# Seven block products in place of eight in the up-projections of a feed-forward layer

## The chip, the cores and the metric

The program runs on one core of a Trainium2 chip. Five engines work beside each other, each through its own queue in a fixed order: TensorE (PE in the profile, with PEld for the loads of its stationary operands), VectorE (DVE), ScalarE (ACT), GpSimd (POOL) and SyncE (SP), which here only issues DMAs. The metric is the device time of one execution in microseconds (us): the median of several runs.

## The reference

One inference step of an encoder trunk with two layers, over 640 tokens: 512 frames of a new stream, and 16 frames each of 8 running streams. The width is 1024. The first layer mixes by chunked spatial gating beside a gated convolution, the second by attention with forget gates. Each layer then has a feed-forward part, and that is what the change is about. All in float32:

```python
def _conv_ffn(x, prev, w_up, conv_w, w_down):       # x is normed; w_up (1024, 5632), w_down (2816, 1024)
    z, st = _causal_dwconv(x @ w_up, conv_w, prev)   # width 3, along time; prev: the streams' last two rows
    gate, up = jnp.split(z, 2, axis=-1)
    return (jax.nn.silu(gate) * up) @ w_down, st
...
    hp = _rmsnorm(xp, norm_ffn[layer])
    yp, st_p = _conv_ffn(hp, zero_f, w_up[layer], conv_ffn[layer], w_down[layer])
    xp = xp + yp
```

The same is done for the running streams, with their states. The last rows of `x @ w_up` are outputs too, as the new state.

## The kernel before

**Layout.** Activations are kept with features on the 128 partitions and tokens along the free axis: `x` is 8 chunks of 128x640. Weights are the stationary operand of TensorE, tokens move. A product of a float32 weight and a float32 activation is made of three float32r products: each operand is split into a high part (a cast) and a low part (what the cast left out), and high x high, high x low and low x high are accumulated in PSUM. A matmul has 320 tokens, half of them all, and the two halves lie on the two sides of a PSUM bank border. So one output block of 128 features costs 8 chunks x 3 x 2 = 48 matmuls.

**Weights.** `weights()` (L83 to L90) loads 128x1024 float32 (512 KB) by a DMA that SP issues into `raw` (L87), casts the high part `whi` on ACT (L88) and subtracts the low part `wlo` on DVE (L89). Each of the three has a ring of three buffers.

**The norm.** The operands `hh` and `hl` of the up-projection are x times the norm's gain g only. The root `rb`, a number for each token, is multiplied in when a product leaves PSUM.

**The feed-forward layer.** `ffn()` walks over 22 units. Unit j (`up(j)`) is output block j of the gate and block 22+j of the up half: 96 matmuls (L109). Then, for each of the two blocks, `pad_evac` takes the block from PSUM times `rb` into a padded buffer `zp` (DVE L190, L191; POOL L183 puts the old state in), `new_state` copies the last two columns of each stream (POOL L202), and `conv` makes three taps (ACT L196, DVE L198 twice). The gate goes through silu (ACT L355); the product (DVE L358, L359) is split again (ACT L97, DVE L98) and becomes an operand of the down-projection.

The down-projection is done in parts, since its contraction runs over all units: `PARTS` lists units 0 to 5, 6 to 11, 12 to 16 and 17 to 21. After each part (and the first unit of the next) `project` runs through the eight output blocks, with 6 matmuls for each unit of the part, and adds each block to x (DVE L209). The block that ends the program is halved by tokens (`last_block`, L327).

**PSUM.** The pool `pm` has three tiles of two banks, tag `mm`; two more banks are the pool behind `aux()`.

**What sets the order.** A scheduler walks through the program as written, with a model of durations, and writes a fixed order for each engine's queue. On the chip each queue runs in that order; semaphores make it wait for the others. An instruction that waits holds back everything behind it in its own queue.

Of the kernel before, what the change touches and what calls it, by code (L numbers as in the profile page):

```python
# [8 lines left out]
F32 = mybir.dt.float32  # L9
# [34 lines left out]
# columns of the constants of the attention  # L44
# [4 lines left out]
NS = 256 + 16      # keys of a stream  # L49


class Core:
    def __init__(self, ctx, tc, io):
# [5 lines left out]
        self.wp = pool(ctx, "wts", bufs=3)  # L59
        self.hp = pool(ctx, "hp", bufs=8)  # L60
        # 4 norms x 8 chunks
# [8 lines left out]
        self.n = 0  # L70

# [4 lines left out]
    # ---- weights: float32 from DRAM, split exactly into two float32r parts  # L76
    def weights(self, src, cols=1024, pieces=1, between=None):
        nc = self.nc
        raw = self.wp.tile([P, 1024], F32, tag="raw", name=self.nm("raw"))
# [12 lines left out]
    def split(self, pool, tags, src):  # L92
        """float32 [128, 640] -> (hi, lo) float32r tiles"""
        nc = self.nc
        hi = pool.tile([P, T], F32R, tag=tags[0], name=self.nm("sh"))
        lo = pool.tile([P, T], F32R, tag=tags[1], name=self.nm("sl"))
        nc.scalar.copy(out=hi, in_=src)  # L97
        nc.vector.tensor_tensor(out=lo, in0=src, in1=hi.bitcast(F32), op=ALU.subtract)  # L98
        return hi, lo

    # ---- products, weights stationary, tokens moving
# [10 lines left out]
    def psum(self):  # L112
        return self.pm.tile([P, 1024], F32, tag="mm", name=self.nm("mm"))
# [11 lines left out]
    # ---- RMS norm: operands scaled by g now, by the root later  # L125
# [28 lines left out]
    def stats(self, acc, pool, aux):  # L154
        """1/rms for each token, as columns [128, 5]"""
# [8 lines left out]
    def spread(self, rt, pool, aux):  # L164
        """columns [128, 5] -> the same along the free axis of every partition"""
# [727 lines left out]
```

## Time and profile before

| | |
|---|---|
| median of 3 runs | 1534.07 us (1534.03 to 1534.29) |
| the profiled execution's span, first to last instruction | 1531.9 us |
| granted TensorE clock in it, mean | 1.000 |
| first mixer | to about 200 us |
| feed-forward of layer 0 | about 227 to 680 us |
| attention | about 680 to 1076 us |
| feed-forward of layer 1 | about 1076 to 1532 us |

The profile is of one execution, 2.2 us shorter by its span than the median. Its page gives the busy time of each engine, the chain of work that ended last and the groups of instructions by line. A view of waits lists what an engine waited for; a view by stretches gives busy times within a stretch; a timeline lists single instructions with start and length. In the names of instructions stands output <- inputs, then partitions x elements.

### The profile page before, as it was taken

The numbers are of one execution on the slowest core, as the hardware profiler recorded it, in microseconds if no ns is written. First come the engines' busy times: TensorE is split into PE (matmuls) and PEld (weight loads), VectorE is DVE, ScalarE is ACT, GpSimd is POOL, SyncE is SP. The second block draws the span as 40 slices with busy tenths as digits, with TensorE's granted clock in tenths as the row PEclk, the third lists the DMA queues.
The fourth block names the chain that finished last, engine by engine and source line by source line (L and its number), as shares of the span: only waits on it lengthen the run. The fifth ranks groups of instructions, "written<-read, shape, count | busy, mean of one in ns | idle before, by whom it ended". The sixth has DMA issues, their size and how long they took to land.

```text
span 1531.9 us, 26648 instructions
## 1 busy us (share of the span) xinstructions
PE 1517.8 (99%) x11008; PEld 1473.5 (96%) x11008; DVE 899.1 (59%) x1541; ACT 559.4 (37%) x918; POOL 237.4 (15%) x281
## 2 busy tenths in 40 slices
PE   8999999999999999999999999999999999999999
PEld 6999999999999999999989888888999999999998
DVE  6545437644653655675676766768765466365463
ACT  5422334322322322345545454535432233133231
POOL 5000122201210201143111111003221021021010
PEclk9999999999999999999999999999999999999999
DMA  6222212222223222243544343523222222321313
GB/s 226 77 82 73 77 56 85 68 81 85 62 64 95 64 66 93 62 156 103 180 128 136 122 123 104 183 60 107 83 60 76 87 67 57 98 73 53 107 47 106
DMA packets 52296, 142.90 MB, mean 93 GB/s; under 512 B 6656, under 2 KB 13744, under 8 KB 52048
## 3 DMA queue, kind: packets, MB, share of 16 engines
q1 hardware_dynamic: 45424, 133.79, 28.6%
q10 hardware_dynamic: 6752, 7.41, 1.4%
q8 instruction: 87, 1.43, 0.4%
q14 instruction: 33, 0.27, 0.1%
HBM read 125.41 MB, written 11.54 MB: 89 GB/s over the span
## 4 chain that ended last, share of the span: by engine, by line
PE 96%; DVE 2%; issue 1%; ACT 1%; DMA 0%; POOL 0%; SPq 0%; DVEq 0%; ACTq 0%
PE mm L109 71%; PE pj L507 10%; PE pv L583 3%; PE po L109 2%; PE pt L576 1%; PE mm L239 1%; PE pt L662 1%; PE sc L569 1%; DVE hl L132 1%; PE sc L570 1%; DVE wlo L89 1%; PE scs L641 1%; PE pt L537 1%; PE pt L655 0%; PE scs L634 0%
## 5 line engine op out<-in xcount | busy, mean ns | idle before, releaser
L88 ACT CAST whi<-raw 128x1024 fp32r<-128x1024 f32 (+4 forms) x222 | 207.6, 937 | 494.6 <-PE mm L109 426.1
L109 PE MATMUL mm<-hl,whi 128*128 128x320 f32 x1664 | 379.4, 309 | 0.5 <-DVE hl L132 0.5
L109 PE MATMUL mm<-hh,whi 128*128 128x320 f32 x1664 | 379.8, 309 | 0.0
L109 PE MATMUL mm<-hh,wlo 128*128 128x320 f32 x1664 | 379.2, 309 | 0.0
L109 PEld LDWEIGHTS mm<-hl,whi 128*128 128x128 f32 x1664 | 278.2, 188 | 0.7 <-DVE hl L132 0.7
L109 PEld LDWEIGHTS mm<-hh,whi 128*128 128x128 f32 x1664 | 278.2, 188 | 0.1
L109 PEld LDWEIGHTS mm<-hh,wlo 128*128 128x128 f32 x1664 | 278.0, 188 | 0.0
L89 DVE TENSOR_TENSOR wlo<-raw,whi 128x1024 fp32r<-128x1024 f32 (+4 forms) x222 | 245.5, 1107 | 33.3 <-ACT whi L88 33.0
L109 PE MATMUL mm<-sh,wlo 128*128 128x320 f32 x866 | 197.2, 309 | 1.3 <-DVE wlo L89 1.3
L109 PE MATMUL mm<-sl,whi 128*128 128x320 f32 x866 | 197.2, 309 | 0.0
L109 PE MATMUL mm<-sh,whi 128*128 128x320 f32 x866 | 196.2, 309 | 0.0
L202 POOL COPY so<-zp 128x18 f32<-128x18 f32 x88 | 89.4, 1016 | 570.4 <-DVE zp L191 570.4
L190 DVE TENSOR_TENSOR zp<-mm,rb 128x512 f32<-128x512 f32 x88 | 60.9, 692 | 195.8 <-PE mm L109 195.8
L209 DVE TENSOR_TENSOR x<-mm,x 128x640 f32<-128x640 f32 x79 | 65.0, 823 | 185.6 <-PE mm L109 185.6
L198 DVE SCALAR_TENSOR_TENSOR t<-zp,cst,t 128x656 f32<-128x656 f32 x184 | 165.1, 900 | 10.3 <-ACT t L196 5.6
L109 PEld LDWEIGHTS mm<-sh,wlo 128*128 128x128 f32 x866 | 144.6, 188 | 1.6 <-DVE wlo L89 1.6
L109 PEld LDWEIGHTS mm<-sl,whi 128*128 128x128 f32 x866 | 144.8, 188 | 0.0
L109 PEld LDWEIGHTS mm<-sh,whi 128*128 128x128 f32 x866 | 144.4, 188 | 0.2 <-issue 0.2
L507 PE MATMUL pj<-wlo,hh 128*128 128x256 f32 x480 | 137.7, 287 | 0.7 <-DVE wlo L89 0.7
L507 PE MATMUL pj<-whi,hh 128*128 128x256 f32 x480 | 137.7, 287 | 0.0
L507 PE MATMUL pj<-whi,hl 128*128 128x256 f32 x480 | 137.5, 287 | 0.0
L507 PEld LDWEIGHTS pj<-wlo,hh 128*128 128x128 f32 x480 | 91.6, 191 | 2.8 <-issue 1.6
(188 smaller groups left out, 1691.3 us busy)
## 6 DMA issues: line engine op xcount, KB each, us to landing
raw<-w_up SPq DMA_DIRECT2D x88, 512.0 KB
raw<-w_dn SPq DMA_DIRECT2D x32, 384.0 KB
raw<-w_c SPq DMA_DIRECT2D x24, 512.0 KB
raw<-w_dn SPq DMA_DIRECT2D x32, 320.0 KB
raw<-w_ab SPq DMA_DIRECT2D x16, 512.0 KB
ck<-c_k SPq DMA_DIRECT2D x16, 512.0 KB
cv<-c_v SPq DMA_DIRECT2D x16, 512.0 KB
o_kv<-z ACTq DMA_DIRECT2D x8, 640.0 KB
```

Source lines behind the costliest of these rows:

```text
L88: nc.scalar.copy(out=hi[:, c], in_=raw[:, c])
L89: nc.vector.tensor_tensor(out=lo[:, c], in0=raw[:, c], in1=hi[:, c].bitcast(F32), op=ALU.subtract)
L109: nc.tensor.matmul(outs[h], lhsT=l, rhs=r[:, h * HT:(h + 1) * HT], start=start and k == 0, stop=stop and k == 2)
L132: nc.vector.scalar_tensor_tensor(out=lo, in0=x, scalar=gs, in1=hi.bitcast(F32), op0=ALU.mult, op1=ALU.subtract)
L190: nc.vector.tensor_tensor(out=op, in0=a[:, 0:TP], in1=b[:, 0:TP], op=ALU.mult)
L198: nc.vector.scalar_tensor_tensor(out=cv[:, 0:CW], in0=zp[:, i:i + CW], scalar=w[:, i:i + 1], in1=cv[:, 0:CW], op0=ALU.mult, op1=ALU.add)
L202: self.nc.gpsimd.tensor_copy(out=out.rearrange("p (s c) -> p s c", c=2), in_=zp[:, 496:ZW].rearrange("p (s c) -> p s c", c=18)[:, :, 16:18])
L209: self.nc.vector.tensor_tensor(out=x, in0=ps[:, C0:C0 + T], in1=x, op=ALU.add)
L239: nc.tensor.matmul(pvs[tb], lhsT=l[:, tb * P:(tb + 1) * P], rhs=r[:, (kc % 2) * 512:(kc % 2 + 1) * 512], start=kc == 0 and k == 0, stop=kc ...
L507: nc.tensor.matmul(out[tb], lhsT=l[:, tb * P:(tb + 1) * P], rhs=r[:, c:c + 256], start=kc == 0 and i == 0, stop=kc == 7 and i == 2)
L537: nc.tensor.transpose(t[:, tb * P:(tb + 1) * P], z[i][:, tb, pair * P:(pair + 1) * P], k.ident)
L583: nc.tensor.matmul(ov[64 * hh:64 * hh + 64, i * P:n], lhsT=z[2][:, j, (2 * pair + hh) * 64:(2 * pair + hh) * 64 + 64], rhs=u[:, j * P:(j + ...
```

## The change

The four quarters of a pair of output blocks are computed with seven products in place of eight (a form of Winograd's variant of Strassen's scheme). A unit is the matrix [gate block, up block] over K = 1024, and the moving matrix has two halves of tokens. K is cut in two by chunks: `KORD` puts the even chunks into the first half and the odd ones into the second, and `_layout` orders the rows of `w_up` so. Each product is over 4 chunks, one 320-token operand and one set of weights: 4 x 3 = 12 matmuls, 84 for the unit in place of 96.

- **Operands.** The scheme needs sums and differences of the two token halves, so the operands must be fully normed (x times g times `rb`). Units 0 to 3 (`NSTD`) stay standard, on the old operands, while `forms(j)`, written after each unit, makes two normed chunks (DVE L144) and four combinations of 320 tokens for them (DVE L148 to L151); three combinations are split into `fbh` and `fbl`. At unit 4 `settle` overwrites the old operands with the splits of the normed chunks.
- **Weights.** `pair_weights` loads the gate block (`g`) and the up block with its two halves of K swapped (`u`), splits D from the first half of `u`, then adds two more blocks from DRAM into `u` by an accumulating DMA that POOL issues (L172; the copies `w_x` are new inputs, made beside the others by reordering alone), and makes two sums on DVE (L175, L176). A, B and C are splits of 1024 columns.
- **Low parts by DMA.** `added` (L101 to L105) makes a low part as minus the high part on ACT (L103), to which a POOL-issued accumulating DMA adds the unsplit value (L104). It serves the weights of units 1 to 3 (`weights_added`), the down blocks (`weights_down`) and `fbl`. Unit 0 still uses `weights()`.
- **PSUM.** Banks X, Z and Y of a unit; ACT copies values out in between (`snap`, L204), and DVE combines them into the padded buffers (L211, L219, L220, L222). The pool `pm` becomes `pz` (two tiles) and `pd` (one); `psum()` takes turns among the three.
- **Order.** Six parts (0-3, 4-7, 8-11, 12-15, 16-18, 19-21). From unit 4 the down blocks of the previous part are written between the products of the units (`downs.pop`); the last part keeps `project`.
- **The rest.** `new_state` moves from POOL to ACT (L340). There are three `zp` instead of four, 4 `tmp`, four buffers of `whi` and `wlo`; `rb` shares a buffer with `acc`. The scratch space of GpSimd's DMAs is set to 1024.

The core of the diff:

```diff
-PARTS = ((0, 6), (6, 12), (12, 17), (17, 22))
+PARTS = ((0, 4), (4, 8), (8, 12), (12, 16), (16, 19), (19, 22))
+NSTD = 4
+KORD = (0, 2, 4, 6, 1, 3, 5, 7)
...
+    def added(self, pool, tags, raw, src, n, cols):
+        nc = self.nc
+        hi, lo = (pool.tile([P, n], F32R, tag=t, name=self.nm(t)) for t in tags)
+        nc.scalar.copy(out=hi[:, 0:cols], in_=raw)
+        nc.scalar.mul(out=lo[:, 0:cols], in_=hi[:, 0:cols].bitcast(F32), mul=-1.0)
+        nc.gpsimd.dma_start(out=lo[:, 0:cols], in_=src, accum_op=ALU.add)
+        return hi, lo
+    def weights_added(self, src):
+        raw = self.raw()
+        self.nc.sync.dma_start(out=raw, in_=src)
+        return self.added(self.wp, ("whi", "wlo"), raw, src, 1024, 1024)
+    def weights_down(self, src, cols):
+        raw = self.fx.tile([P, 512], F32, tag="dr", name=self.nm("dr"))[:, 0:cols]
+        self.nc.sync.dma_start(out=raw, in_=src)
+        return self.added(self.fd, ("dh", "dl"), raw, src, 512, cols)
...
+    def forms(self, p, x, g, rb, ring, fb):
+        ys = [pool.tile([P, T], F32, tag=t, name=self.nm("y")) for t in tags]
+        for c, y in zip((2 * p, 2 * p + 1), ys):
+            stt(out=y, in0=x[c], scalar=self.gv[:, 8 * g + c:8 * g + c + 1], in1=rb, op0=ALU.mult, op1=ALU.mult)
+        (a1, b1), (a2, b2) = ((y[:, 0:HT], y[:, HT:T]) for y in ys)
+        t = self.raw()[:, 0:3 * HT]
+        t2, t3, t4 = (t[:, i * HT:(i + 1) * HT] for i in range(3))
+        tt(out=t3, in0=b2, in1=b1, op=ALU.subtract)
+        tt(out=b1, in0=a1, in1=b1, op=ALU.subtract)
+        stt(out=t2, in0=b2, scalar=-1.0, in1=b1, op0=ALU.mult, op1=ALU.subtract)
+        stt(out=t4, in0=t2, scalar=-1.0, in1=a2, op0=ALU.mult, op1=ALU.subtract)
+        return ys, self.added(fb, ("fbh", "fbl"), t, t, 3 * HT, 3 * HT)
+    def settle(self, p, h, form):
+        ys, fb = form
+        for y, (hi, lo) in zip(ys, h):
+            self.part(hi, lo, y)
...
+    def pair_weights(self, gate, up, more):
+        g, u, v = self.raw(), self.raw(), self.raw()
+        nc.sync.dma_start(out=g, in_=gate)
+        nc.sync.dma_start(out=u, in_=up)
+        D = self.split(self.fd, ("dh", "dl"), u[:, 0:H], H)
+        nc.gpsimd.dma_start(out=u, in_=more, accum_op=ALU.add)
+        A = self.split(self.wp, w, g, 1024)
+        B = self.split(self.wp, w, u, 1024)
+        nc.vector.tensor_tensor(out=v[:, 0:H], in0=u[:, 0:H], in1=g[:, 0:H], op=ALU.add)
+        nc.vector.tensor_tensor(out=v[:, H:2 * H], in0=g[:, H:2 * H], in1=v[:, 0:H], op=ALU.add)
+        C = self.split(self.wp, w, v, 1024)
...
+    def pair_blocks(self, w, f, zg, zu, states, downs):
+        self.product(X, w["x11"], f, "y1a", True)
+        p1 = snap(X, 1.0)
+        self.product(Z, w["x12"], f, "y2a", True)
+        nc.vector.tensor_tensor(out=zg[:, 2:2 + HT], in0=Z, in1=p1, op=ALU.add)
+        self.product(X, w["s2"], f, "t2", False)
+        u = snap(X, -1.0)
+        self.product(Y, w["s3"], f, "t3", True)
+        p7 = snap(Y, -1.0)
+        if downs:
+            downs.pop(0)()
+        self.product(X, w["s1"], f, "t1", False)
+        nc.vector.tensor_tensor(out=zu[:, 2 + HT:514], in0=p7[:, 0:n], in1=X[:, 0:n], op=ALU.subtract)
...
+        self.product(Y, w["x22"], f, "t4", False)
+        nc.vector.tensor_tensor(out=zu[:, 2:2 + HT], in0=u, in1=Y, op=ALU.subtract)
+        if downs:
+            downs.pop(0)()
+        self.product(X, w["s4"], f, "y2b", False)
+        nc.scalar.copy(out=zg[:, 2 + HT:514], in_=X[:, 0:n])
...
+            for j in range(a, b):
...
+                if j < NSTD:
+                    blocks = (j, NJ + j)
+                    if j == 0:
+                        ps = self.blocks([self.weights(io["w_up"][l, i]) for i in blocks], hk, first)
+                    else:
+                        ps = [self.blocks([self.weights_added(io["w_up"][l, i])], hk)[0] for i in blocks]
...
+                else:
+                    if f is None:
+                        f = [self.settle(p, (h[2 * p], h[2 * p + 1]), forms[p]) for p in range(4)]
+                    w = self.pair_weights(io["w_up"][l, j], io["w_x"][l, j, 0], io["w_x"][l, j, 1])
+                    self.pair_blocks(w, f, zg, zu, sts, downs)
...
+                acts.append(act(zg, zu, j))
+                if j < NSTD:
+                    forms.append(self.forms(j, x, g, rb, ring, fb))
```

How the order moves is shown at the start of the first feed-forward layer. Before, ACT's queue around the end of unit 0 (`whi_264`, `whi_267` are the weights of unit 1, `whi_277`, `whi_280` those of unit 2; the L196 and L355 rows are unit 0's convolutions and silu):

```order
L88 CAST whi_267_2137<-raw_266_2136 128x1024
L88 CAST whi_277_2265<-raw_276_2264 128x1024
L196 ACTIVATE t_258_2110<-zp_2_88,cst_66 128x656
L196 ACTIVATE t_259_2119<-zp_4_90,cst_66 128x656
L355 ACT_TABLE_LOAD
L355 ACTIVATE t_258_2110<-t_258_2110 128x656
L88 CAST whi_280_2271<-raw_279_2270 128x1024
L97 CAST sh_261_2126<-t_260_2123 128x640
```

Here the casts of the weights of unit 1, and one of unit 2, stand ahead of the work on unit 0's products. After the change, ACT's queue from the end of unit 1 to the start of unit 2 (`zp_4` and `zp_2` hold unit 1's blocks, `whi_291` and `whi_295` are unit 2's weights):

```order
L340 COPY so_253_2004<-zp_2_88 128x18
L334 ACTIVATE t_280_2274<-zp_2_88,cst_66 128x656
L334 ACTIVATE t_281_2278<-zp_4_90,cst_66 128x656
L483 ACTIVATE t_281_2278<-t_281_2278 128x656
L127 CAST sh_283_2286<-t_282_2283 128x640
L102 CAST fbh_288_2299<-raw_287_2294 128x960
L102 CAST whi_291_2306<-raw_290_2304 128x1024
L103 ACTIVATE fbl_289_2300<-fbh_288_2299 128x960
L102 CAST whi_295_2362<-raw_294_2360 128x1024
L103 ACTIVATE wlo_292_2307<-whi_291_2306 128x1024
L103 ACTIVATE wlo_296_2363<-whi_295_2362 128x1024
```

The casts of unit 2's weights now stand behind unit 1's convolutions, silu, split and `fbh`, the cast of its combined operands. What `fbh` reads is made on DVE, in this order after the convolution of unit 1:

```order
L486 TENSOR_TENSOR t_282_2283<-t_281_2278,t_280_2274 128x512
L487 TENSOR_TENSOR t_282_2283<-t_281_2278,t_280_2274 128x128
L144 SCALAR_TENSOR_TENSOR y_285_2290<-x2_76,gv_64,rb_244_1974 128x640
L128 TENSOR_TENSOR sl_284_2287<-t_282_2283,sh_283_2286 128x640
L144 SCALAR_TENSOR_TENSOR y_286_2291<-x3_77,gv_64,rb_244_1974 128x640
L148 TENSOR_TENSOR raw_287_2294<-y_286_2291,y_285_2290 128x320
L149 TENSOR_TENSOR y_285_2290<-y_285_2290 128x320
L150 SCALAR_TENSOR_TENSOR raw_287_2294<-y_286_2291,y_285_2290 128x320
L151 SCALAR_TENSOR_TENSOR raw_287_2294<-raw_287_2294,y_286_2291 128x320
```

The two normed chunks (L144), which read only x, the gain and `rb`, stand behind the product of the unit. And PE after the change, from the last matmuls of unit 1 (`mm_279`) into unit 2 (`mm_293` and `mm_297`):

```order
L239 MATMUL mm_279_2217<-hh_239_1957,whi_277_2212 128x320 x2
L239 MATMUL mm_279_2217<-hl_240_1958,whi_277_2212 128x320 x2
L239 MATMUL mm_279_2217<-hh_239_1957,wlo_278_2213 128x320 x2
L239 MATMUL mm_293_2311<-hh_195_1573,whi_291_2306 128x320 x2
L239 MATMUL mm_293_2311<-hl_196_1574,whi_291_2306 128x320 x2
L239 MATMUL mm_297_2367<-hh_195_1573,whi_295_2362 128x320 x2
L239 MATMUL mm_297_2367<-hl_196_1574,whi_295_2362 128x320 x2
L239 MATMUL mm_293_2311<-hh_195_1573,wlo_292_2307 128x320 x2
```

Unit 2 begins with eight matmuls on the high parts of both its blocks, then needs the low part `wlo_292`. Nothing of another unit stands between. In all, PE has 10576 matmuls in place of 11008.

More of the change, by code (lines that the diff above doesn't have):

```diff
@@ L70, in __init__ @@
         self.n = 0
+        self.turn = -1
     def nm(self, s):
@@ new lines, in weights_added, with split @@
+    def weights_added(self, src):
+        raw = self.raw()
+        self.nc.sync.dma_start(out=raw, in_=src)
[4 more added lines that the diff above has]
+        return self.added(self.fd, ("dh", "dl"), raw, src, 512, cols)
+    def split(self, pool, tags, src, n=T):
+        nc = self.nc
+        hi = pool.tile([P, n], F32R, tag=tags[0], name=self.nm("sh"))
+        lo = pool.tile([P, n], F32R, tag=tags[1], name=self.nm("sl"))
+        self.part(hi, lo, src)
+        return hi, lo
@@ L201, in new_state @@
     def new_state(self, zp, out):
[L202 to L203 removed]
+        self.nc.scalar.copy(out=out.rearrange("p (s c) -> p s c", c=2),
+                            in_=zp[:, 496:ZW].rearrange("p (s c) -> p s c", c=18)[:, :, 16:18])
     def conv_compact(self, cv):
@@ new lines, in ffn, with act @@
+        two = lambda a, n: a.rearrange("p (u c) -> p u c", u=2)
+        def act(zg, zu, b):
+            cvs = []
+            for z, i in ((zu, 1), (zg, 0)):
+                o = O_CF + (l * NB + b + i * NJ) * 3
+                cv = self.conv(z, self.cst[:, o:o + 3])
+                if i == 0:
+                    nc.scalar.activation(out=cv[:, 0:CW], in_=cv[:, 0:CW], func=AF.Silu)
+                cvs.append(self.conv_compact(cv))
+            pr = self.tmp()
+            nc.vector.tensor_tensor(out=pr[:, 0:TP], in0=cvs[1][0], in1=cvs[0][0], op=ALU.mult)
+            nc.vector.tensor_tensor(out=pr[:, TP:T].rearrange("p (s c) -> p s c", c=16), in0=cvs[1][1], in1=cvs[0][1], op=ALU.mult)
+            return self.split(rpool, rtags, pr[:, :T])
@@ L375 @@
+        self.project([io["w_dn"][l, ob][:, a * P:b * P] for ob in range(8)], prev, None, x, finish, cols=(b - a) * P, out=out)
 class Attention:
@@ L810, in _layout @@
     d["w_oab"] = cols(a["w_out_ab"][0], 8)
-    d["w_up"] = np.stack([cols(a["w_up"][l], NB) for l in range(2)])
+    wu = np.stack([cols(a["w_up"][l].reshape(NC, P, -1)[list(KORD)].reshape(1024, -1), NB) for l in range(2)])
+    d["w_up"] = wu
+    up, gate = wu[:, NJ:], wu[:, :NJ]
+    d["w_x"] = con(np.stack([np.concatenate([up[..., 512:], up[..., :512]], -1),
+                             np.concatenate([up[..., :512], gate[..., :512]], -1)], 2))
     d["w_dn"] = np.stack([cols(a["w_down"][l], 8) for l in range(2)])
```

164 lines of the change are left out of this document (105 added, 59 removed).

## The prediction

> **What bounds the kernel now.** I read the busy shares first, then the chain that ended last, then what TensorE (PE) waited for, and then the feed-forward stages alone.
>
> ```profile
> span 1531.9 us, 26648 instructions
> PE 1517.8 (99%) x11008; PEld 1473.5 (96%) x11008; DVE 899.1 (59%) x1541; ACT 559.4 (37%) x918; POOL 237.4 (15%) x281
> PE 96%; DVE 2%; issue 1%; ACT 1%; DMA 0%; POOL 0%; SPq 0%; DVEq 0%; ACTq 0%
> ```
>
> PE works 99% of the span and carries 96% of the chain. The pieces of the chain and the waits of PE say how tightly:
>
> ```profile
> 125.26 7.04 PE mm L109 x48
> 227.19 452.76 PE mm L109 x3087
> 1076.18 447.33 PE mm L109 x3050
> ...
> PE mm L239 <- ACT hh L131: 5.7, 1, 5.7
> PE mm L239 <- DVE wlo L89: 1.6, 1, 1.6
> PE mm L109 <- DVE wlo L89: 1.3, 1, 1.3
> ```
>
> Both feed-forward stages (227 to 680 us and 1076 to 1523 us) are one unbroken run of matmuls of 128x320. The first is 452.76 us for 3087, or **146.67 ns a matmul**; one block of 48 alone, 7.04 us, gives the same. All waits of PE that are listed sum to about 11 us, half of it at the program's start. So a matmul taken out of these stages is worth its whole 146.67 ns, and a new wait of PE there costs its whole length. The view by stages shows how much room the other engines have in the first stage (the columns are the stretch, then busy us and count for PE, PEld, DVE, ACT, POOL, then granted clock, DMA share and GB/s):
>
> ```profile
> 227.00:680.00 453.00, 453.00 (x3091) 453.00 (x3090) 262.07 (x356) 151.59 (x181) 73.04 (x90) 1.00 0.27 81
> ```
>
> DVE is busy 58% of it, ACT 33%, POOL 16%, the DMA engines 27%.
>
> **The change part by part.** *Matmuls removed.* In 36 units (18 in each layer) 96 matmuls become 7 products of 12, so 12 fewer each: 432 x 146.67 ns = **-63.4 us**. The products stay at 128x320 and in PSUM, and the blocks of 48 above already show that pace within one block, so I price a remaining matmul as before.
>
> *Units from the fifth on.* A unit there has 84 matmuls and, with its share of the previous part's down blocks (eight over four units, so two blocks of 24 matmuls), 132: 19.4 us. DVE and ACT get more kinds of work, but these rows price it:
>
> ```profile
> L89 DVE TENSOR_TENSOR wlo<-raw,whi 128x1024 fp32r<-128x1024 f32 x140 | 173.3, 1240 | 28.6 <-ACT whi L88 28.3
> L198 DVE SCALAR_TENSOR_TENSOR t<-zp,cst,t 128x656 f32<-128x656 f32 x184 | 165.1, 900 | 10.3 <-ACT t L196 5.6
> L88 ACT CAST whi<-raw 128x1024 fp32r<-128x1024 f32 x140 | 146.7, 1049 | 325.7 <-PE mm L109 264.9 <-issue 39.6 <-PE aux L239 10.7
> L209 DVE TENSOR_TENSOR x<-mm,x 128x640 f32<-128x640 f32 x79 | 65.0, 823 | 185.6 <-PE mm L109 185.6
> L97 ACT CAST sh<-t 128x640 fp32r<-128x640 f32 x52 | 37.8, 727 | 137.6 <-DVE t L359 120.8 <-DVE t L279 9.5 <-DVE t L300 7.3
> L358 DVE TENSOR_TENSOR t<-t,t 128x512 f32<-128x512 f32 x44 | 30.5, 693 | 1.7
> L774 DVE TENSOR_TENSOR x<-po,x 128x320 f32<-128x320 f32 x16 | 7.4, 486 | 1.3 <-PE po L109 1.1
> ```
>
> DVE: three subtractions of 1024 and one of 512, two sums of 512, four evacuations of up to 320, four convolution steps, the product, one split and two additions to x: 3.7+0.7+1.4+1.7+3.6+1.0+0.8+1.6 = 14.5 us, 75% of 19.4. ACT: four casts, five copies of PSUM, two convolution starts, silu, the split and two down blocks at two casts each: about 12 us, 63%. Neither becomes the bound. Every wait that the order gives PE there has cover: the addition of `more` into `u` (L172) has 53 to 121 matmuls of earlier work between its release and its reader (mostly 71 or more, 10 us), the low parts of the down blocks 65 or more (9.5 us). The raw buffers turn over in about 12.2 us plus one accumulating transfer, against 19.4 us. I price the units at nothing, as long as such a transfer takes under 7 us; without that cover each microsecond above it costs one in each of 36 units.
>
> *Units 0 to 3.* Here the change adds a wait. In the order of ACT, the cast of the high part of the next unit's weights (L102 `whi`) now stands **behind** the cast of the unit's combined operands (`fbh`), which waits for the end of a chain on DVE: evacuation of the unit, convolution, silu, product, two normed chunks (L144) and four combinations (L148 to L151). Nothing else is left for PE: all that stands behind the unit's last matmul reads those weights. Before, the casts for the next unit stand ahead of the unit's own convolutions, and PE goes straight on. This happens at four places a layer, after units 0, 1, 2 and 3. How long that chain is can be read from the same steps in this trace (start, length):
>
> ```profile
> 306.93 0.69 DVE L190 TENSOR_TENSOR zp<-mm,rb 128x512 f32<-128x512 f32 x1 [0.79 <-PE mm L109]
> 307.54 0.28 DVE L191 TENSOR_TENSOR zp<-mm,rb 128x128 f32<-128x128 f32 x1
> ...
> 307.92 0.85 ACT L196 ACTIVATE t<-zp,cst 128x656 f32<-128x656 f32 x1 [0.47 <-DVE zp L191]
> 310.67 0.75 ACT L355 ACTIVATE t<-t 128x656 f32<-128x656 f32 x1 [1.91 <-DVE t L198]
> ```
>
> From the unit's last matmul: start of the evacuation 0.25 (my estimate of the handoff, the gaps between engines in these rows being 0.1 to 0.25); the evacuation to the start of ACT 1.0 (306.93 to 307.92); the state's copy on ACT, which stands in front, 0.2; one convolution start 0.85; four steps on DVE at 0.9, 3.6; silu 0.75; product 0.9 (starts 0.61 apart, then 0.28). That is 7.5. The product's split waits for ACT (0.73), the first normed chunk fills that time; subtraction 0.82 and second chunk 0.88, so 9.9. Four combinations of 320 elements at 0.49: 11.9. Cast of 960 elements, about 1.0: 12.9. Then `whi`, 1.05: 14.0, and the first matmul at 14.3. Eight matmuls on high parts alone follow, then PE needs `wlo`: ACT does `fbl` 1.0, the second `whi` 1.05, the negation 1.05, to 17.3; then the accumulating DMA of 512 KB takes L. **The stall is 17.3 + L - 8 x 0.147 = 16.1 + L**, at three transitions a layer.
>
> *L* is not in this trace. The nearest rows are a plain load:
>
> ```profile
> 0.74 0.38 SPq L87 DMA_DIRECT2D raw<-w_v  x1
> 3.43 0.62 ACT L88 CAST whi<-raw 128x512 fp32r<-128x512 f32 x1 [0.76 <-DMA raw<-w_v]
> q1 hardware_dynamic: 45424, 133.79, 28.6%
> ```
>
> 256 KB issued at 0.74 are used at 3.43, 2.7 us; the queue's 133.79 MB in 28.6% of the span (438 us) are 305 GB/s, so 512 KB take 3.5 us. That is the lower bound. If adding makes every byte count twice, 1.8 us of fixed part and 1 MB are 5.3 us; and the addition for `fbl` (480 KB) stands ahead on the same queue, which would bring it to about 9, the upper bound. I take the middle case, twice the bytes and little queueing, **L = 5.5**: 6 x 21.6 = **+129.6 us**. The Trainium skill's DMA: Bandwidth & Descriptors (Anatomy of one DMA) fits a transfer issued from GpSimd with 2.0 us plus bytes at 436 GB/s, 3.2 us for 512 KB, and says nothing of the second read; with that estimate the whole sum below would be 18 us lower.
>
> *Into unit 4* the first products also wait: `settle` splits the eight normed chunks on ACT and DVE, and `more` is added before its sums and splits. Following the order, `more` has landed at 16.1 + L, the splits that the sixth product reads end 6.8 later, and 60 matmuls (8.8 us) are done meanwhile: stall 14.1 + L = 19.6, twice, **+39.2 us**.
>
> *The clock after a stall.* The one place of this trace where PE starts after several idle microseconds is the program's start (matmuls of 512 columns):
>
> ```profile
> 5.68 1.22 PE L239 MATMUL mm<-whi,hh 128*128 128x512 f32 x2 [5.68 <-ACT hh L131]
> 7.13 0.63 PE L239 MATMUL mm<-whi,hl 128*128 128x512 f32 x1
> 7.55 0.63 PE L239 MATMUL mm<-wlo,hh 128*128 128x512 f32 x1
> ...
> 13.10 0.39 PE L239 MATMUL mm<-wlo,hh 128*128 128x512 f32 x1
> 13.33 0.39 PE L239 MATMUL mm<-whi,hl 128*128 128x512 f32 x1
> ```
>
> The first twelve follow each other at 0.427 us (7.13, 7.55), later ones at 0.227 (13.10, 13.33). From 5.68 to 10.54 that costs 4.9 - 12 x 0.227 = 2.1 us. Bounds for each of the eight stalls: 0 and 2.1. I take 2.1, the only row there is: **+16.8 us**. The rule that fits is in the Trainium skill's TensorE: Matmul & The Clock Gate (The HAM clock gate): after an idle window of about 3.4 us the clock is halved until the array has been busy for as long; the rows agree, with half the pace for 4.9 us.
>
> *The rest.* The last part's down blocks share one PSUM buffer behind the last pair unit, with short windows of 5 to 18 matmuls against an addition to x of 0.82 us and its handoffs: about **+4 us** for both layers, bounds 0 and 8. The copies of the new state, 1.0 us on POOL before, go to ACT at about 0.2 and are in the chain above. The first mixer and the attention keep their work; its one buffer fewer of padding I price at nothing, since POOL and DVE have the room shown.
>
> **Sum:** 1531.9 - 63.4 + 129.6 + 39.2 + 16.8 + 4 = 1658.1 us of span. The median of the runs is 2.2 us above the profiled span (1534.07 against 1531.9), so **1660 us**.
>
> **The rivals.** *The accumulating DMAs bind the pair units too.* Every pair unit has one of 512 KB and two of 256 KB on one queue, issued by POOL in order; L is unknown, and nothing in the trace shows two of them overlapping. With L = 9 the stalls grow by 3.5 each (+28), and the turnover of the raw buffers, 12.2 + 9 = 21.2 us, passes 19.4: +1.8 in 36 units, +65. That gives about 1750. Against it: the DMA engines stand at 27%. *The stalls are shorter.* L = 3.5, no slow restarts, and a chain that overlaps by 1.5 us more than I sum: 1660 - 16 - 17 - 12 = 1615. For it: the intervals above include waits of this kernel. *Faster: the chain does not reach PE.* If the next unit's weights came without the operands' chain ahead of them, each transition would cost only what was left of L. The point from which it decides is a stall of (63.4 - 4)/8 = 7.4 us a transition, without slow restarts: below it the change wins. Covered fully, the time is 1534.1 - 63.4 + 4 = 1475. For it speaks only that the chain is made of my own sums; against it that the order of ACT is fixed, and that the steps on DVE before `fbh` alone (four convolution steps, the product, two chunks, one subtraction, four combinations) take 9.1 us. *The change doesn't do what it says* would need PE to have as many matmuls as before; the order has 432 fewer.
>
> **How the numbers follow.** My forecast, 1660, holds with 0.62; the DMA-bound case 0.18; the shorter stalls 0.12; faster 0.06; a balance within 0.2% 0.02. The range reaches down past the shorter stalls, to 1595 (a stall of about 12 us a transition with no slow restarts: 1474.7 + 8 x 15), and up to 1745, nearly the DMA-bound case. About 0.2% (3 us) is what a measurement of this kernel can tell from no change. Slower holds the forecast, the DMA case and the short stalls: 0.92.
>
> **What would show it.** Right: eight gaps of PE, after units 0 to 3 of each layer, each in two pieces, about 14 us that end on ACT's `whi` (L102) and 6 to 9 us that end on the accumulating DMA into `wlo`; 10576 matmuls, PE's share near 90%; matmuls at twice their spacing for some microseconds behind each gap; pair units without gaps. Wrong: gaps under 8 us, or gaps spread over the pair units, ended by `more` or by a down block's `dl`.

## The result, and the profile after

The changed kernel takes **1729.5 us** (median of 4 runs, 1726.31 to 1734.64) against 1534.18 us for the kernel before on the same chip: a ratio of 1.1277, 95% interval 1.1257 to 1.1298. The forecast was 1660 us, within 1595 to 1745. The profiled execution spans 1728.3 us, 196.4 more than the one before. Its page, the same parts that the prediction quotes of before:

```profile
span 1728.3 us, 26656 instructions
PE 1515.7 (88%) x10576; PEld 1442.8 (83%) x10576; DVE 999.6 (58%) x1721; ACT 756.6 (44%) x1418; POOL 270.3 (16%) x323
PEclk9999977679999999999999999996677999999999
PE 56%; DMA 17%; DVE 13%; issue 9%; ACT 5%; POOL 1%; ACTq 0%; SPq 0%; DVEq 0%; POOLq 0%
```

PE has its 432 matmuls fewer, and is busy for only 2.1 us less. The clock, full throughout before, falls to 0.6 and 0.7 in two places, and a sixth of the chain is now DMA. The waits of PE (total us, times, longest):

```profile
PE mm L239 <- ACT whi L102: 83.6, 12, 13.5
PE mm L239 <- DMA wlo<-w_up: 44.9, 6, 8.0
PE zx L189 <- ACT sh L127: 25.8, 2, 12.9
PE aux L189 <- ACT sh L127: 14.5, 8, 3.1
```

The timeline of PE shows the gaps after unit 0 and into unit 4 of layer 0 (start, length of one, and in brackets the wait and what ended it):

```profile
244.40 0.90 PE L239 MATMUL mm<-hh,whi 128*128 128x320 f32 x2 [13.54 <-ACT whi L102]
...
246.24 0.90 PE L239 MATMUL mm<-hh,whi 128*128 128x320 f32 x2 [0.41 <-ACT whi L102]
...
255.39 0.90 PE L239 MATMUL mm<-hh,wlo 128*128 128x320 f32 x2 [7.71 <-DMA wlo<-w_up]
...
362.38 0.63 PE L189 MATMUL zx<-hh,sh 128*128 128x320 f32 x1 [12.90 <-ACT sh L127]
```

What stands ahead on DVE, ACT and POOL in the first of them:

```profile
241.88 0.49 DVE L151 SCALAR_TENSOR_TENSOR raw<-raw,y 128x320 f32<-128x320 f32 x1
...
242.41 0.99 ACT L102 CAST fbh<-raw 128x960 fp32r<-128x960 f32 x1 [3.79 <-DVE raw L151]
243.31 1.04 ACT L102 CAST whi<-raw 128x1024 fp32r<-128x1024 f32 x1
...
247.45 1.80 POOL L104 DMA_DIRECT2D wlo<-w_up  x2 [0.79 <-ACT wlo L103]
```

The last combination on DVE, then `fbh`, then `whi`, then PE at 244.40: the chain that the prediction summed. And the stages (stretch, then busy us and count for PE, PEld, DVE, ACT, POOL, then clock, DMA share, GB/s):

```profile
228.00:380.00 152.00, 72.54 (x377) 67.22 (x377) 53.63 (x83) 46.52 (x65) 15.89 (x24) 0.67 0.32 74
380.00:774.00 394.00, 375.93 (x2504) 369.18 (x2503) 255.82 (x359) 201.47 (x362) 69.80 (x92) 0.99 0.56 128
...
1179.00:1330.00 151.00, 71.23 (x374) 66.06 (x373) 53.61 (x83) 46.85 (x65) 15.15 (x21) 0.68 0.32 73
1330.00:1728.30 398.30, 376.85 (x2502) 369.72 (x2500) 249.95 (x356) 192.63 (x349) 61.74 (x88) 0.99 0.54 124
```

The first and third row hold the four transitions of a layer, the second and fourth its pair units. From these rows, against before:

| term | forecast, us | measured, us | from |
|---|---|---|---|
| matmuls removed | -63.4 | -63.4 | 432 at 146.67 ns, a pace shown below |
| six transitions, units 0 to 3 | +129.6 | +128.5 | 83.6 + 44.9 |
| into unit 4, twice | +39.2 | +30.7 | PE idle in rows 1 and 3 (79.5 + 79.8), less 128.5 |
| pair units and the end | +4 | +35.8 | PE idle in rows 2 and 4 (39.5 together), less 3.7 in the last stage before |
| matmuls that take longer | +16.8 | +61.3 | busy 1515.7 against 1517.8 - 63.4 |
| idle elsewhere | 0 | +3.5 | the rest of PE's idle time |

The sum is 196.4. Of the 61.3 us, 33.6 lie in rows 1 and 3 and 18.6 in rows 2 and 4; the other 9 are outside these rows (busy time less count times 146.67 ns; a matmul that ends before a wait is booked a little longer than one that another follows, so not all of it is the clock).

### The profile page after: what moved, and what is told of

Its sections match the earlier page's. It is cut to its first block, busy times and chain, and to the rows that moved or that the text cites. A ratio compares the mean times of both kernels' runs of the same rounds, so it can differ in the third digit from the quotient of the medians.

```text
span 1728.3 us, 26656 instructions
## 1 busy us (share of the span) xinstructions
PE 1515.7 (88%) x10576; PEld 1442.8 (83%) x10576; DVE 999.6 (58%) x1721; ACT 756.6 (44%) x1418; POOL 270.3 (16%) x323
## 4 chain that ended last, share of the span: by engine, by line
PE 56%; DMA 17%; DVE 13%; issue 9%; ACT 5%; POOL 1%; ACTq 0%; SPq 0%; DVEq 0%; POOLq 0%
PE mm L239 23%; DMA raw<-w_x 11%; PE pj L672 10%; PE zx L189 7%; DVE t L336 3%; PE aux L189 3%; DMA wlo<-w_up 3%; PE pv L748 2%; PE po L239 2%; DVE sl L128 2%; DMA dr<-w_dn 2%; PE pt L741 1%; ACT sh L127 1%; DVE x L347 1%; DMA dl<-w_dn 1%
## 5 line engine op out<-in xcount | busy, mean ns | idle before, releaser
L127 ACT CAST sh<-raw 128x1024 fp32r<-128x1024 f32 (+1 forms) x144 | 134.5, 939 | 220.5 <-DMA raw<-w_x 149.8
L189 PE MATMUL zx<-hh,sh 128*128 128x320 f32 x576 | 182.7, 317 | 32.8 <-ACT sh L127 25.8
L239 PE MATMUL mm<-hh,whi 128*128 128x320 f32 x512 | 127.4, 332 | 83.6 <-ACT whi L102 83.6
L128 DVE TENSOR_TENSOR sl<-raw,sh 128x1024 fp32r<-128x1024 f32 (+1 forms) x144 | 155.9, 1088 | 48.3 <-ACT sh L127 48.0
L189 PE MATMUL zx<-hh,sl 128*128 128x320 f32 x576 | 179.8, 316 | 3.6 <-DVE sl L128 3.6
L189 PE MATMUL zx<-hl,sh 128*128 128x320 f32 x576 | 181.2, 315 | 0.0
L239 PEld LDWEIGHTS mm<-hh,whi 128*128 128x128 f32 x512 | 92.4, 204 | 87.7 <-ACT whi L102 87.6
L239 PE MATMUL mm<-hh,wlo 128*128 128x320 f32 x512 | 122.4, 324 | 44.9 <-DMA wlo<-w_up 44.9
L239 PE MATMUL mm<-sh,dh 128*128 128x320 f32 x608 | 140.6, 312 | 4.2 <-DVE x L347 4.1
L239 PE MATMUL mm<-sh,dl 128*128 128x320 f32 x608 | 139.9, 309 | 0.9 <-DMA dl<-w_dn 0.9
L239 PE MATMUL mm<-sl,dh 128*128 128x320 f32 x608 | 139.9, 310 | 0.0
L104 POOL DMA_DIRECT2D dl<-w_dn x80 | 71.0, 887 | 401.0 <-ACT dl L103 303.1
L239 PEld LDWEIGHTS mm<-hh,wlo 128*128 128x128 f32 x512 | 90.6, 200 | 47.3 <-DMA wlo<-w_up 47.3
L239 PE MATMUL mm<-hl,whi 128*128 128x320 f32 x512 | 124.8, 327 | 0.0
L95 DVE TENSOR_TENSOR wlo<-raw,whi 128x1024 fp32r<-128x1024 f32 (+4 forms) x90 | 96.4, 1073 | 36.8 <-ACT whi L94 36.6
```

The source lines that it names most:

```text
L95: nc.vector.tensor_tensor(out=lo[:, c], in0=raw[:, c], in1=hi[:, c].bitcast(F32), op=ALU.subtract)
L104: nc.gpsimd.dma_start(out=lo[:, 0:cols], in_=src, accum_op=ALU.add)
L189: nc.tensor.matmul(out, lhsT=l[:, c], rhs=r, start=start and p == 0 and i == 0, stop=p == 3 and i == 2, skip_group_check=True)
L239: nc.tensor.matmul(outs[h], lhsT=l, rhs=r[:, h * HT:(h + 1) * HT], start=start and k == 0, stop=stop and k == 2)
```

## The experiments

The theory: PE stands still because ACT makes the next unit's weights behind the forms, and then because the low part comes by an accumulating DMA. The rivals: the accumulating DMAs alone set the end, wherever the casts stand; the pair units are bound by them too; a slow array has another cause than idleness.

**Next unit's weights first.** In the loop over the standard units:

```diff
+                    if j + 1 < NSTD:
+                        nxt = [self.weights_added(io["w_up"][l, i + 1]) for i in blocks]
...
-                        ps = [self.blocks([self.weights_added(io["w_up"][l, i])], hk)[0] for i in blocks]
+                        ps = [self.blocks([w], hk)[0] for w in nxt]
```

(the new lines stand behind `pad_evac`, ahead of the activation and the forms)

> One edit to the changed kernel: the loads, casts and accumulating DMAs of the next standard unit's weights are written before the activation and the combined operands of the unit, so ACT has the first of them ahead of fbh. If the wait sits in that order (my theory), the gap after unit 0 of each layer goes wholly, that after unit 1 becomes a wait for the low part alone (about 10 us, since ACT still makes the negation behind unit 1's convolution and the addition takes about 8 us), that after unit 2 goes too: about 2 x (21.5 + 11 + 21.5) = 108 us less, and some 4 us of slow clock for each gap that is gone, so 1590 to 1625 us against 1729. The rival that the accumulating DMA sets the end wherever the casts stand expects at most the 13.5 us pieces to go (6 x 13.5 = 81) and the pieces of 7.7 us to stay: 1640 to 1650 us or more.

Measured: **1596.4 us** (1595.2 to 1597.5), 133 less. Its PE timeline from 225 us to the first pair unit holds only these waits:

```profile
246.29 0.55 PE L239 MATMUL mm<-hh,whi 128*128 128x320 f32 x2 [1.24 <-ACT whi L102]
249.71 0.90 PE L239 MATMUL mm<-hh,whi 128*128 128x320 f32 x2 [2.57 <-ACT whi L102]
259.30 0.90 PE L239 MATMUL mm<-hh,wlo 128*128 128x320 f32 x2 [8.16 <-DMA wlo<-w_up]
302.62 0.63 PE L189 MATMUL zx<-hh,sh 128*128 128x320 f32 x1 [13.37 <-ACT sh L127]
```

The gaps after units 0 and 2 are gone, and the one after unit 1 is the low part and a few microseconds of `whi`. The order was the cause; the rival that DMAs alone set the end falls.

**Subtraction in units 1 to 3**, the order left as it was:

```diff
-                        ps = [self.blocks([self.weights_added(io["w_up"][l, i])], hk)[0] for i in blocks]
+                        ps = [self.blocks([self.weights(io["w_up"][l, i])], hk)[0] for i in blocks]
```

> One edit to the changed kernel: units 1 to 3 split their weights as before, with a subtraction on DVE in place of the negation on ACT and the accumulating DMA; the order stays with the weights behind the combined operands. My theory: the first piece of each gap (13.5 us, ended by ACT's whi) stays, the second (7.2 to 8.0 us, ended by the DMA into wlo) goes, since the subtraction takes 1.24 us and eight matmuls stand in front of it: 6 x 7.5 = 45 us less, and about 2 us of slow clock for each piece, so 1670 to 1690 us. The rival that it is POOL's queue or the DMA rings as a whole that are late expects the wait to turn up elsewhere, and less than 20 us less.

Measured: **1673.0 us**, 56.5 less. The first piece stays, the second is gone:

```profile
243.11 0.91 PE L239 MATMUL mm<-hh,whi 128*128 128x320 f32 x2 [13.53 <-ACT whi L94]
243.81 0.74 PE L239 MATMUL mm<-hl,whi 128*128 128x320 f32 x2
244.37 0.91 PE L239 MATMUL mm<-hh,wlo 128*128 128x320 f32 x2
```

Behind the gap one pair of matmuls starts 0.56 us after the other (243.81 to 244.37), 0.28 a matmul, half the pace of before.

**The same, with the array kept busy.** The 85 matmuls stand ahead of each of units 1 to 3; `ws` holds the weights of the unit before, and the lines that keep it are left out:

```diff
+                        junk = self.aux()[:, 0:HT]
+                        for _ in range(85):
+                            nc.tensor.matmul(junk, lhsT=ws[1][0][:, 0:P], rhs=hk[0][0][:, 0:HT], start=True, stop=True)
...
```

> The kernel of the subtraction, with 85 matmuls of 128x320 whose result nobody reads put between the units 0 to 1, 1 to 2 and 2 to 3 of each layer (about 12.5 us of work each at full clock, inside a wait of 13.5 us). It computes the same outputs. If the array is slow after a wait because it stood idle, the real matmuls behind the gap now go at their full pace: 3 to 4 us less for each of six gaps, so about 20 us faster than the kernel of the subtraction although it does more work, and a granted clock of 1.00 in these stretches. If the slow stretch has another cause (the operands that arrive late, or contention), the time stays within 5 us of it or grows.

Measured: **1664.8 us** (1662.0 to 1667.6), 8 us less with 510 matmuls more. The same place:

```profile
242.99 0.57 PE L239 MATMUL mm<-hh,whi 128*128 128x320 f32 x2 [1.08 <-ACT whi L94]
...
244.64 0.45 PE L239 MATMUL mm<-hh,whi 128*128 128x320 f32 x2
244.93 0.45 PE L239 MATMUL mm<-hl,whi 128*128 128x320 f32 x2
```

Here it is 0.29 us a pair, full pace, though the operands come as late as before. So it is at two of the six places. At the other four the pace is halved again, behind the same short waits (1.07 us for `whi`, then 0.41 us for `wlo`):

```profile
271.54 0.56 PE L239 MATMUL mm<-hh,whi 128*128 128x320 f32 x2 [1.07 <-ACT whi L94]
...
273.26 0.73 PE L239 MATMUL mm<-hh,whi 128*128 128x320 f32 x2
273.80 0.73 PE L239 MATMUL mm<-hl,whi 128*128 128x320 f32 x2
```

This is 0.54 us a pair. By the starts of the first 40 matmuls behind each wait, less 40 times 146.67 ns, a restart costs 2.1 to 2.9 us in the run before this one; here it is 0.8 us at two places and 2.3 at four. So operands that come late do not by themselves slow the array, and with most of the idle time filled the slow stretches shrink or go; why the same short waits are followed by half pace at four places and not at two, no run tells. That is why the saving stayed below the 20 us expected: from one unit's first matmul to the next one's it is 2.1, 0.6 and 0.6 us in layer 0 and -0.2, 1.7 and 0.4 in layer 1.

**Both: weights first, and subtraction.**

> Both edits: the next unit's weights written before the activation and the forms, and split by subtraction on DVE. My theory: no gap is left between units 0 and 3 but a few microseconds after unit 1; what remains is the start of unit 4 (20 us a layer or more, as two of the forms now stand there) and the waits inside the pair units (about 20 us a layer): 1560 to 1600 us. If the accumulating DMA of fbl and the combined operands themselves hold PE, it stays above 1640.

Measured: **1582.0 us** (1580.1 to 1583.9). No gap over 1.3 us is left between units 0 and 3. What is left against 1470 or so (before, less 63.4) lies at the first pair unit and inside the pair units. The runs that follow start from this kernel, where nothing else is said.

**The blocks for `u` by a plain load and a sum on DVE:**

```diff
-        nc.gpsimd.dma_start(out=u, in_=more, accum_op=ALU.add)
+        nc.sync.dma_start(out=v, in_=more)
+        nc.vector.tensor_tensor(out=u, in0=u, in1=v, op=ALU.add)
```

> On top of the kernel with both edits (weights ahead, subtraction: 1582 us): the blocks that the accumulating DMA adds into u are loaded plainly into the buffer v and added on DVE (1024 elements, about 1.2 us a unit). The theory that the waits inside the pair units (about 18 us a layer) come from ACT's queue standing before the cast of u, which waits 5.5 us for the addition, expects about half of them to go: 1560 to 1575 us. The rival that three raw buffers are the limit expects it to become slower, since v is now taken from its load on and the next unit's loads wait longer: 1590 us or more, with PE waiting for casts of raw data.

Measured: **1534.0 us** (1532.0 to 1534.6, 8 runs), ratio to the kernel before 0.9994, interval 0.9982 to 1.0005, so no difference from it is shown. It is 48 us less than 1582; I had expected 7 to 22. Waits in the kernel with both edits:

```profile
PE zx L189 <- ACT sh L127: 26.7, 2, 13.4
PE aux L189 <- ACT sh L127: 13.1, 10, 3.1
...
ACT sh L127 <- DMA raw<-w_x: 140.3, 43, 7.3
```

and with this edit, where ACT's wait of 140 us is no longer listed among its largest:

```profile
PE zx L190 <- ACT sh L127: 26.8, 2, 13.4
...
PE aux L190 <- ACT sh L127: 2.0, 1, 2.0
```

PE's idle time falls by 25 us (1578.3 - 1493.4 to 1532.8 - 1472.8) and its busy time by 21. **On the changed kernel alone** the edit was tried as well:

> The changed kernel with one edit: the blocks for u are loaded plainly and added on DVE; the waits after units 0 to 3 stay as they are. On the kernel with the weights ahead this edit gave 48 us (1582.0 to 1534.0). If the accumulating transfer binds the pair units by itself, whatever happens at the standard units, the same again: about 1729 - 48 = 1681 us, with the waits of PE after units 0 to 3 unchanged (13.5 and 7.2 to 8.0 us). If the two parts of the loss overlap, less than 35 us.

Measured: **1685.1 us** (1682.9 to 1687.3), 44 less, with the waits for `whi` at 83.6 us as before and those for `wlo` at 46.8. The two losses add up.

**The down blocks' low parts by subtraction on DVE**, in place of L103 and L104 there:

```diff
-        return self.added(self.fd, ("dh", "dl"), raw, src, 512, cols)
+        hi, lo = (self.fd.tile([P, 512], F32R, tag=t, name=self.nm(t)) for t in ("dh", "dl"))
+        self.part(hi[:, 0:cols], lo[:, 0:cols], raw)
+        return hi, lo
```

> On top of the kernel with both edits (1582 us): the low parts of the down blocks are subtracted on DVE in place of the negation on ACT and the accumulating DMA of 256 KB. The queue of POOL loses 80 transfers of about 0.9 us issue and 4.4 us landing, ACT 0.63 us a block, DVE gains about 0.7 us a block, 1.4 us a unit of 19.4. If the accumulating transfers of the down blocks hold the pair units through POOL's queue or the raw buffer of one, 10 to 20 us less; if they are covered, as their windows of 65 matmuls and more say, within 5 us of 1582; if DVE is near its limit, slower.

Measured: **1555.1 us** (1553.7 to 1556.4), 27 less, more than the 10 to 20 expected: these transfers, too, cost time. PE never waited for them by name for more than a microsecond in the changed kernel, so they do so through ACT's or POOL's queue or the DMA engines; which of them, no run tells.

**A fifth standard unit**, and the first pair unit's weights earlier (the call of `pair_weights` for it, left out here, stands ahead of the activation of the unit in front):

```diff
-NSTD = 4
+NSTD = 5
...
-                if j < NSTD:
+                if j < 4:
                     forms.append(self.forms(j, x, g, rb, ring, fb))
```

> On top of the kernel with both edits (1582 us): unit 4 is standard too, while the forms still belong to units 0 to 3, and the weights of the first pair unit are written before the activation of the unit ahead of it. 24 matmuls more (+3.5 us). The wait at the first pair unit (13.4 us and a few small ones behind it, and the slow clock after it) loses the chain of the last unit's activation and forms; what stays are the splits of the normed chunks, which overwrite operands in use until the last standard matmul: 6 to 9 us a layer. 1555 to 1570 us. If the wait there is one for the pair unit's weights and not for the forms, it stays above 1580.

Measured: **1569.8 us** (1568.1 to 1571.4), 12 less, with 24 matmuls more. The wait of 13.4 us is gone in both layers, but the waits of `aux` products for casts grew from 13.1 to 18.0 us, and one of 8.0 us appeared at the start of the attention.

**A fourth raw buffer.** To make room for it, D and the down blocks got three buffers in place of four; a second kernel has that alone.

> On top of the kernel with the weights ahead and subtraction (1582 us, accumulating transfers for u and the down blocks still there): four raw buffers in place of three, and, to make room, three buffers in place of four for D and the down blocks. The trace of the changed kernel shows the turnover of the raw buffers at 19.67 us from one addition into u to the next (581.64 to 601.31), against 19.4 us of matmuls in a unit: landing 5.6, sum 1.4, the next loads 4, ACT's queue and the split 7. If that ring is what binds, a fourth buffer lets the next unit's loads start ahead of the sums and the waits go: 20 to 45 us less than the kernel with three buffers for D and the down blocks alone. If ACT's queue, which stands before the cast of u, is the limit whatever the loads do, less than 10 us.

> The comparison for it: three raw buffers as before, and three buffers in place of four for D and the down blocks. On top of the kernel with both edits (1582 us): within 10 us of it if these buffers were not short; more if they were.

Measured: **1587.6 us** (1583.0 to 1592.1) and **1619.9 us** (1614.7 to 1625.1). The fourth buffer is worth 32 us there, within the 20 to 45 that the turnover of the raw buffers was expected to free. But the comparison was expected within 10 us of 1582, if D and the down blocks had buffers enough, and was 38 above it, with `PE mm L239 <- DMA dl<-w_dn` at 32.3 us: D and the down blocks were short of buffers as well, and the 32 us are measured in that shortage.

**The edits together** (weights first, subtraction in units 1 to 3 and for the down blocks, the load and sum for `u`, the fifth standard unit; the raw buffers as they were):

> All edits together (weights ahead, every low part and the sum for u on DVE, fifth unit standard): no accumulating DMA is left but those of fbl. DVE has about 17 us of work in a pair unit of 19.4. If the waits inside the pair units come from the accumulating transfers, 1530 to 1550 us, near the kernel before; if DVE or the raw buffers become the limit, 1560 us or more.

Measured: **1514.4 us** (1514.1 to 1514.7), ratio 0.9874, interval 0.9845 to 0.9902: 1.3% faster than the kernel before, and 16 us below the best that I expected. **And without any accumulating DMA**, the forms' low parts by subtraction too:

```diff
-        return ys, self.added(fb, ("fbh", "fbl"), t, t, 3 * HT, 3 * HT)
+        return ys, self.split(fb, ("fbh", "fbl"), t, 3 * HT)
```

> The kernel with all edits (1514.4 us) with the last accumulating DMAs, those of fbl, replaced by a subtraction of 960 elements on DVE, eight in all. They are off the path in that kernel, since the forms have a whole unit of time, so the same time within 3 us: 1511 to 1517 us, clearly below the kernel before (1534.1). If DVE, busy 80% in these stretches, is what the first pair unit waits for, up to 5 us slower.

Measured: **1511.3 us** (1509.1 to 1511.9), ratio **0.9848, interval 0.9831 to 0.9864**. One of its stretches of pair units (columns as above):

```profile
400.00:500.00 100.00, 100.00 (x685) 100.00 (x684) 81.12 (x115) 50.36 (x89) 2.82 (x10) 1.00 0.37 117
```

685 matmuls in 100 us are 146.0 ns each: the products and the down blocks between them run unbroken at the pace of before, with DVE busy 81%.

## Why the prediction was right, and where its sizes were off

*The matmuls saved.* Right: 146 ns each in the unbroken stretches, so 63 us were to be had. 24 of the 432 were given back in the last two kernels for the fifth unit.

*The stall of 21.6 us at units 0 to 3.* Right in cause (weights first: minus 133 us) and in sum (128.5 for six), but the sum was in part luck: its parts were off and made up for each other. The chain to the first matmul took 13.5 in place of 14.3 us. The accumulating DMA was later than L = 5.5: from the end of the negation to PE about 8 us. The eight matmuls that I set at 1.2 us ran at half pace and covered nearly 3. The list of DMA issues (queue, count, KB, median us from issue to landing) shows what L depends on:

```profile
raw<-w_x POOLq DMA_DIRECT2D x36, 512.0 KB, 5.5
...
wlo<-w_up POOLq DMA_DIRECT2D x12, 512.0 KB, 8.7
...
fbl<-raw POOLq DMA_DIRECT2D x8, 480.0 KB, 7.0
```

The transfers into `u` land in 5.5 us, the value taken; `fbl` and two `wlo`, issued one behind the other within 3 us, land in 7.0 to 8.7, near the upper bound of 9. The Trainium skill's DMA: Bandwidth & Descriptors (Anatomy of one DMA) gives 3.2 us for this size, as an estimate by its fit. The accumulating transfers of 512 KB here took 5.5 and 8.7 in the median, so the measurement decides against using that fit for them.

*Into unit 4.* Near in size, 15.4 in place of 19.6 us, but by luck: I had hung the sum on the addition of `more` and put the wait at the sixth product. The wait stands at the first product. It ends on the cast of the pair unit's own weights (ACT L127, 12.9 us), which stands in ACT's queue behind unit 3's activation and the casts of the last normed chunks.

*The clock.* Right in mechanism and near in the price of one restart (2.1 us, against the 2.1 to 2.9 of the subtraction run), wrong in number. Each of the six transitions has two waits, of 13.5 us and of 7.1 to 8.0, and half pace follows both: 33.6 us of longer matmuls in the eight stretches in place of 16.8. And the pair units have slow stretches too. The Trainium skill's TensorE: Matmul & The Clock Gate (The HAM clock gate) puts the halving of the clock behind an idle window of about 3.4 us. The waits of 7 us and more agree with that; that half pace followed waits of 1.07 and 0.41 us at four places of the busy-array run does not come out of such a rule.

*The pair units, priced at nothing.* **This is the step that failed.** "The raw buffers turn over in about 12.2 us plus one accumulating transfer, against 19.4 us" gave 17.7 with L = 5.5, a margin of 1.7 us. One turn in the changed kernel, from one addition into `u` to the next:

```profile
581.64 0.87 POOL L172 DMA_DIRECT2D raw<-w_x  x1 [1.68 <-DVE sl L128]
...
601.31 0.88 POOL L172 DMA_DIRECT2D raw<-w_x  x1 [1.42 <-DVE sl L128]
```

and what it consists of on ACT:

```profile
587.25 1.05 ACT L127 CAST sh<-raw 128x1024 fp32r<-128x1024 f32 x1 [5.67 <-DMA raw<-w_x]
...
595.68 0.62 ACT L102 CAST dh<-dr 128x512 fp32r<-128x512 f32 x1 [2.73 <-DMA dr<-w_dn]
...
597.60 1.55 ACT L127 CAST sh<-raw 128x512 fp32r<-128x512 f32 x2
```

This turn took 19.67 us, no margin: 5.6 to the landing of the addition, 1.4 for the sums, then loads, the cast of D that stands behind a cast which waits for a down block's load, and D's subtraction, which DVE reached only at 600.22. What I had put at 12.2 us, all but the addition, took 14.1. The 17 turns of this layer vary from 16.5 to 35.4 us, with a mean of 20.8. Since a turn is also the time of a unit, its length alone does not say what binds; the runs that took the transfer away or gave a fourth buffer do. How the addition reaches PE shows ahead of the longest wait of layer 0 behind its first pair unit, 3.08 us to 610.79:

```profile
606.84 0.69 DVE L175 TENSOR_TENSOR raw<-raw,raw 128x512 f32<-128x512 f32 x1 [3.99 <-DMA raw<-w_x]
...
608.38 0.75 ACT L483 ACTIVATE t<-t 128x656 f32<-128x656 f32 x1 [7.67 <-DVE t L336]
...
609.69 1.04 ACT L127 CAST sh<-raw 128x1024 fp32r<-128x1024 f32 x1 [0.55 <-issue]
```

DVE stands until the addition has landed, and the convolution that the silu on ACT needs stands behind it; the cast that PE waits for stands behind the silu. So the latency of the transfer came back through two in-order queues. The prediction held this addition for covered by 53 matmuls and more, 7.8 us, between its release and its reader; here it is 9.5 us from the issue (601.31) to the reader (610.79). Taking the transfer away gave 44 to 48 us, of the 36 of idle time and 19 of longer matmuls in these stages; how much of it belongs to the buffers and how much to the queues, no run separates. The rival in which the accumulating DMAs bind the pair units had the place right and the price near (65), though with L = 9, where L was 5.5 and the rest of the turnover longer.

So the time came out 70 us above the forecast, within the range, and 20 below the 1750 of that rival, to which I had given 0.18. Of the 70 us, 32 are the pair units and 44 the longer matmuls. Both kinds of sign that I had named came: six of the eight gaps in their two pieces, and against that gaps in the pair units, which by name end on ACT and DVE and not on the transfers. The lower end of the range has a slip: 1595 goes with 15 us a transition, as in its sum, not with the 12 written beside it. The rival "faster" named its condition rightly, the next weights without the chain ahead of them, but not that the pair units had to be freed as well: with the weights first the time was 1596, and 1582 with subtraction, against its 1475.

## What to carry to other kernels

A saving of matmuls is only worth its time if every operand of the next piece of work is made ahead of the chain that hangs on the present one: read the in-order queue of the engine that makes them, and ask what the instruction in front of them waits for. A ring of buffers that turns over within a tenth of the period is not hidden, it is the next bound: sum its loop with every queue that it passes. Moving a low part from an engine that is 58% busy to an accumulating DMA traded 1.2 us of work for 5 to 9 us of latency on three queues, and DVE had the room: all of it fitted, at 72% of the span and 81% in the stretch of pair units shown.

## What the runs showed of the hardware that I had not expected

Waits of PE far shorter than those between the units can slow the array as well, and the length of a wait does not settle it. In the changed kernel a single wait of 3.08 us is followed by full pace, and its twin in layer 1, of 3.15 us, by half pace for 3.5 us. In the run with the next weights first, one of 3.34 us is followed by full pace. Two waits of 2.25 and 0.94 us within 4 us are followed by 5 us at half pace:

```profile
610.79 0.41 PE L189 MATMUL aux<-fbh,sh 128*128 128x320 f32 x1 [3.08 <-ACT sh L127]
611.04 0.31 PE L189 MATMUL aux<-fbl,sh 128*128 128x320 f32 x1
611.18 0.31 PE L189 MATMUL zx<-fbh,sh 128*128 128x320 f32 x1
...
700.71 0.42 PE L189 MATMUL aux<-fbh,sh 128*128 128x320 f32 x1 [2.25 <-ACT sh L127]
...
702.22 0.63 PE L189 MATMUL zx<-hh,sh 128*128 128x320 f32 x1 [0.94 <-ACT sn L204]
702.65 0.47 PE L189 MATMUL zx<-hl,sh 128*128 128x320 f32 x1
...
707.72 0.42 PE L189 MATMUL aux<-fbh,sl 128*128 128x320 f32 x1
...
1557.69 0.51 PE L189 MATMUL aux<-fbh,sh 128*128 128x320 f32 x1 [3.15 <-ACT sh L127]
1557.99 0.47 PE L189 MATMUL aux<-fbl,sh 128*128 128x320 f32 x1
1558.26 0.47 PE L189 MATMUL zx<-fbh,sh 128*128 128x320 f32 x1
```

Between 702.65 and 707.72 there are 19 starts, 0.27 us apart, as are those behind 1557.99; at 611 they are 0.14 apart. With the waits of 1.07 and 0.41 us in the busy-array run, which half pace followed at four places of six, no length of a wait divides the two cases here; what does, the runs do not show. It fits that the plain load, which took 25 us of PE's waits away, took 46 us off the span, though no run separates the two.
